# One decoder layer on one core: the last 1,024 rows of the input projection as one stretch, the gated recurrence ahead of the attention, half of the second modulation on VectorE

## Chip, cores and metric

The kernel runs on one core of a Trainium2 chip. The metric is the device time of one execution in microseconds, the median of several runs. All weights are float32 and come from HBM; every weight is used once.

## What is computed

One layer for 256 tokens of width 2048. `c` is one vector; `mod` gives six rows of 2048, each from 2048 x 2048 weights (16 MiB).

```python
mod = silu(c) @ w_ada + b_ada
sh1, sc1, g1, sh2, sc2, g2 = split(mod, 6)
h = rmsnorm(x, norm1_g) * (1 + sc1) + sh1
hq, hf, hi, hg, q_a, kv_a, k_pe = split(h @ w_in)      # 2048 x 4928
o_a = rmsnorm(hgrn2(hq, hf, hi)) * silu(hg)            # gated recurrence, 8 heads
o_b = rmsnorm(attention(q_a, kv_a, k_pe))              # low-rank q and kv up-projections, 8 heads
x = x + g1 * (concat(o_a, o_b) @ w_out)                # 2048 x 2048
h2 = rmsnorm(x, norm2_g) * (1 + sc2) + sh2
x = x + g2 * moe(h2)       # 32 experts, two per token, gate/up/down 2048 x 512
```

## The kernel before

All large weights pass through one ring of SBUF buffers of 2 MiB. A list `items` gives their order; `ring_fill` issues the loads on SP's queue in that order, `ring_get` takes a chunk, `ring_done` gives its buffer back, and the next load is then issued. The ring has four buffers, two more from `close_temps` on and a seventh once the splits' memory is free.

The kinds of items are: `ad1`, the modulation sh1/sc1 for two K tiles a pair of chunks, by TensorE; `adt`, the same for one K tile, by VectorE, in two passes of 128 x 2048 over transposed weights (`adt_chunk`); `ada`, one eighth of one of g1, sh2, sc2, g2 by TensorE (`ada_chunk`, L293), closed by `ada_end`; `wh` and `win`, the input projection for a pair of column blocks; `qup`/`kvup` for half of the attention heads; `wout` for the output projection; then `gu` and `dn` of the experts.

The input projection has ten column blocks in five pairs: (2,3) and (4,5) are the first half of the recurrence's inputs, (6,7) and (8,9) the second, (0,1) those of attention. Its 16 K tiles go in steps: K tiles 0, 1 and 2, 3 (`wh`, all pairs), then 4 to 7, 8 to 11 and 12 to 15 (`win`). `make_h` prepares h for two K tiles as soon as their modulation is known. `dense` does the matmuls: each weight block of 128 x 512 is divided by ScalarE and VectorE into a high and a low part (a split, L417 and L418, four in flight), and six matmuls (twelve at half the width, L425 to L427) use it. After every step the two sums in PSUM are copied or added to `proj` in SBUF (L455, L457).

The order around the change: K tiles 8 to 11 of all pairs, interleaved with `adt`, then for K tiles 12 to 15 the pair (0,1), which starts `mla_pre`, then `qup`/`kvup` 0 (`mla(0)`), (2,3), (4,5), which starts the first recurrence `hgrn(0)`, `mla(1)`, (6,7), (8,9) and `hgrn(1)`. Between them stand the `ada` chunks; `SPREAD` says how many behind each. The output projection takes the attention half of its rows first (`w_out`, half 0), and the recurrence half second. The last three g2 chunks run behind the output projection, while the router is computed; the first experts' chunks stand ahead of them in the ring. The instructions of each engine are ordered by the framework's scheduler from priorities, so that work of later items can stand among that of earlier ones; each engine then works its own line in order.

Of the kernel before, what the change touches and what calls it, by code (L numbers as in the profile page):

```python
# [45 lines left out]
def tile_hybrid_layer(ctx, tc, A, out):  # L46
# [37 lines left out]
    def bc(ap, shape):  # L84
# [20 lines left out]
    ad1 = [("ad1", h, c) for h in range(2) for c in range(2)]  # L105
    adt = [("adt", kt) for kt in range(4, 16)]
    mods = [("ada", b, ch) for b in ("g1", "sh2", "sc2", "g2") for ch in range(8)]
    last = [[("win", 3, (0, 1))], [("qup", 0), ("kvup", 0), ("win", 3, (2, 3))], [("win", 3, (4, 5))],
            [("qup", 1), ("kvup", 1), ("win", 3, (6, 7))], [("win", 3, (8, 9))]]
    last += [[("wout", 0, j)] for j in range(4)]  # L110
    items = ad1[:2]

    def merge(ws, bs):

        done = 0
        for i, w in enumerate(ws):
            items.append(w)
            want = min(len(bs), -(-(i + 1) * len(bs) // len(ws)))
            items.extend(bs[done:want])
            done = want  # L120

    merge([("wh", 0, p) for p in pairs], ad1[2:])
    merge([("wh", 1, p) for p in pairs], adt[:4])
    for q in range(1, 3):
        merge([("win", q, p) for p in pairs], adt[4 * q:4 * q + 4])
    late_mods = iter(mods)
    items = [x for i, it in enumerate(items) for x in [it] + [next(late_mods) for _ in range(EARLY.get(i, 0))]]
    for ws, n in zip(last + [[("wout", 1, j)] for j in range(4)], SPREAD):
        items += ws + [next(late_mods) for _ in range(n)]
    g2 = list(late_mods)  # L130
    experts = [(k, e, q) for e in range(NE) for k, q in (("gu", 0), ("gu", 1), ("gu", 2), ("gu", 3), ("dn", 0), ("dn", 1))]
    items += experts[:HEAD] + g2 + experts[HEAD:]
    index = {it: i for i, it in enumerate(items)}

    def source(it):
# [5 lines left out]
        if k == "wh":  # L141
            if it[2] == (0, 1):
                return A["w_in_1h"][it[1]], 1664
            return A["w_in_h"][it[1], it[2][0] // 2 - 1], 2048
        if k == "ada":
            return A["w_ada"][("g1", "sh2", "sc2", "g2").index(it[1]), it[2]], 4096
        if k == "win":
            if it[2] == (0, 1):
                return A["w_in_1"][it[1] - 1], 3328
            return A["w_in"][it[1] - 1, it[2][0] // 2 - 1], 4096  # L150
# [1056 lines left out]
```

## Time and profile before

| | us |
|---|---|
| median of 3 runs | 1505.96 (1504.96 to 1506.98) |
| the profiled execution | 1505.27 |
| its span | 1503.0 |
| TensorE busy | 1127.9 (75%) |
| VectorE busy | 588.6 (39%) |
| ScalarE busy | 338.4 (23%) |
| DMA, mean | 383 GB/s, 575.61 MB |

The span counts from the first to the last instruction on the core. Shares are means over stages that differ: the dense layers with the modulation fill the first 570 us, the experts the rest. Busy times of matmuls overlap, as they are pipelined: a 512-wide matmul lasts 0.40 us in the records and the next starts 0.23 us after it.

### The profile page before, as it was taken

To read this page: it belongs to the slowest core of one execution; us is meant where nothing else is said; L and a number is where in the kernel's file an instruction comes from. 1 tells how busy PE (TensorE), PEld (TensorE's weight loads), DVE (VectorE), ACT (ScalarE), POOL (GpSimd) and SP (SyncE) were. 2 spreads that over 40 slices of the span, in tenths; PEclk is the share of its full clock that TensorE was granted. 3 is DMA by queue.
4 is the path that set the end of the run, shared out by engine and by line. 5 is a ranking of instruction groups with operands and counts; after the bars stand their busy time and mean duration, and the time that the engine had idled before them with its cause. 6 is when DMAs were issued, how large, how long until landed. Compare 5 with 4: busy or idle time off the path is not lost.

```text
span 1503.0 us, 22846 instructions
## 1 busy us (share of the span) xinstructions
PE 1127.9 (75%) x9893; PEld 687.8 (46%) x9893; DVE 588.6 (39%) x1200; ACT 338.4 (23%) x699; POOL 5.0 (0%) x9
## 2 busy tenths in 40 slices
PE   5989999979999989675666666657657756666556
PEld 2868887737568756333323323323423423332222
DVE  4699998769765552220120121113112112112112
ACT  5634446536435423000100100100100100000000
POOL 0000000000000000000000000000000000000000
PEclk7999999989999999888888888879888889779787
DMA  9788796877979798999999999999999999999995
GB/s 373 263 332 356 298 352 257 315 302 313 369 293 376 293 373 343 430 429 430 430 430 430 430 430 429 429 431 430 430 430 430 430 431 430 430 429 429 431 430 222
DMA packets 44143, 575.61 MB, mean 383 GB/s; under 512 B 4858, under 2 KB 5114, under 8 KB 8712
## 3 DMA queue, kind: packets, MB, share of 16 engines
q1 hardware_dynamic: 42496, 570.56, 91.4%
q10 hardware_dynamic: 1544, 3.56, 0.6%
q8 instruction: 79, 1.29, 0.3%
q14 instruction: 24, 0.20, 0.0%
HBM read 572.00 MB, written 2.11 MB: 382 GB/s over the span
## 4 chain that ended last, share of the span: by engine, by line
DMA 51%; PE 37%; DVE 9%; ACT 1%; issue 1%; SPq 0%; ACTq 0%; DVEq 0%
DMA wch<-in_w_gu_dram 37%; DMA wch<-in_w_down_dram 13%; PE pgu L1040 5%; PE pacc L433 5%; PE pacc L434 5%; PE pacc L432 5%; PE pada L293 3%; PE py L1016 3%; PE pcmb L993 2%; PE pgat L970 2%; DVE wch L271 2%; DVE split L418 2%; DVE proj L457 1%; PE pacc L427 1%; PE pacc L425 1%; PE pacc L426 1%
## 5 line engine op out<-in xcount | busy, mean ns | idle before, releaser
L1040 PE MATMUL pgu<-wch,XT 128*32 128x256 f32 x4096 | 309.7, 455 | 201.0 <-DMA wch<-in_w_gu_dram 201.0
L1040 PEld LDWEIGHTS pgu<-wch,XT 128*32 128x32 f32 x4096 | 139.2, 126 | 361.0 <-DMA wch<-in_w_gu_dram 253.9
L1016 PE MATMUL py<-wch,hT 128*32 128x256 f32 x2048 | 167.9, 485 | 76.8 <-DMA wch<-in_w_down_dram 72.1
L1020 DVE TENSOR_TENSOR Y<-py,gate 32x256 f32<-32x256 f32 x256 | 107.6, 420 | 216.5 <-PE py L1016 213.6
L1005 DVE TENSOR_TENSOR hid<-sgu,pgu 128x128 f32<-128x128 f32 x32 | 9.2, 287 | 462.2 <-ACT sgu L1003 462.2
L418 DVE TENSOR_TENSOR split<-wch,split 128x512 fp32r<-128x512 f32 (+2 forms) x248 | 159.5, 666 | 69.6 <-ACT split L417 69.0
L417 ACT ACTIVATE split<-wch 128x512 fp32r<-128x512 f32 (+2 forms) x248 | 148.0, 614 | 161.2 <-PE pacc L434 98.4
L1016 PEld LDWEIGHTS py<-wch,hT 128*32 128x32 f32 x2048 | 78.9, 133 | 155.0 <-issue 60.8
L1003 ACT ACTIVATE sgu<-pgu 128x128 f32<-128x128 f32 x32 | 8.9, 277 | 602.5 <-PE pgu L1040 602.5
L975 ACT ACTIVATE XT<-pgat,sh,a 128x128 f32<-128x128 f32 x128 | 48.1, 456 | 223.1 <-PE pgat L970 223.0
L433 PE MATMUL pacc<-split,hhi 128*128 128x512 f32 (+1 forms) x192 | 75.5, 393 | 7.0 <-DVE split L418 7.0
L425 PE MATMUL pacc<-hhi,split 128*128 128x256 f32 x256 | 72.4, 286 | 2.8 <-ACT hhi L388 2.2
L426 PE MATMUL pacc<-hlo,split 128*128 128x256 f32 x256 | 72.7, 285 | 1.7 <-DVE hlo L389 1.7
L434 PE MATMUL pacc<-split,hlo 128*128 128x512 f32 (+1 forms) x192 | 73.7, 386 | 0.0
L432 PE MATMUL pacc<-split,hhi 128*128 128x512 f32 (+1 forms) x192 | 72.9, 392 | 0.8 <-DVE proj L457 0.7
L427 PE MATMUL pacc<-hhi,split 128*128 128x256 f32 x256 | 72.2, 285 | 1.1 <-DVE split L418 1.1
L293 PE MATMUL pada<-wch,ca 128*1 128x512 f32 x512 | 68.7, 602 | 3.3 <-DVE pada L288 3.3
L993 PE MATMUL pcmb<-Y,pwt 128*128 128x512 f32 x128 | 59.2, 605 | 15.5 <-DVE Y L1020 15.5
L970 PEld LDWEIGHTS pgat<-ohr,x 128*128 128x128 f32 x512 | 63.4, 205 | 10.7 <-issue 9.8
L970 PE MATMUL pgat<-ohr,x 128*128 128x128 f32 x512 | 66.8, 291 | 0.7 <-DVE sm L937 0.7
L271 DVE SCALAR_TENSOR_TENSOR wch<-wch,gate 128x2048 f32<-128x2048 f32 x24 | 54.8, 2284 | 0.0
L457 DVE TENSOR_TENSOR proj<-proj,pacc 128x512 f32<-128x512 f32 (+1 forms) x80 | 51.2, 662 | 0.8 <-PE pacc L434 0.4
(311 smaller groups left out, 1215.4 us busy)
## 6 DMA issues: line engine op xcount, KB each, us to landing
wch<-in_w_gu_dram SPq DMA_DIRECT2D x128, 2048.0 KB, 31.1
wch<-in_w_down_dram SPq DMA_DIRECT2D x64, 2048.0 KB, 31.5
wch<-in_w_ada_dram SPq DMA_DIRECT2D x36, 2048.0 KB, 10.1
wch<-in_w_ada_t_dram SPq DMA_DIRECT2D x12, 2048.0 KB, 7.9
wch<-in_w_in_dram SPq DMA_DIRECT2D x12, 2048.0 KB, 9.2
wch<-in_w_out_dram SPq DMA_DIRECT2D x8, 2048.0 KB, 9.5
wch<-in_w_in_h_dram SPq DMA_DIRECT2D x8, 1024.0 KB, 8.9
wch<-in_w_in_dram SPq DMA_DIRECT2D x3, 1664.0 KB, 7.0
```

The lines of the kernel that those rows point to most:

```text
L293: PE.matmul(acc[b][32 * j:32 * j + 1, :], ca[:, kt:kt + 1], w[:, o:o + 512], start=kt == 0, stop=kt == 15)
L417: S.activation(s[:, 0, :ncol], w, AF.Copy)
L418: V.tensor_sub(s[:, 1, :ncol], w, s[:, 0, :ncol])
L426: PE.matmul(o, s[:, 0, c], lo, start=False, stop=False, skip_group_check=True)
L432: PE.matmul(o, hi[:, c], s[:, 0, :ncol], start=first, stop=False)
L433: PE.matmul(o, hi[:, c], s[:, 1, :ncol], start=False, stop=False)
L434: PE.matmul(o, lo[:, c], s[:, 0, :ncol], start=False, stop=stop)
L970: PE.matmul(ps[:, 128 * i:128 * i + 128], x2[kt // 4][:, t, 128 * (kt % 4):128 * (kt % 4) + 128], ohr[:, t], start=t == 0, stop=t == 1)
L993: PE.matmul(ps, PWT[G4][:, 128 * t:128 * t + 128], Y4[j // 2][:, 512 * (j % 2):512 * (j % 2) + 512], start=True, stop=True)
L1016: PE.matmul(py[32 * j:32 * j + 32, :256], H["T"][:, 32 * kt:32 * kt + 32], w[:, 1024 * kt + 256 * j:1024 * kt + 256 * j + 256], start=kt = ...
L1020: V.tensor_mul(Y[q][r:r + 32, 256 * j:256 * j + 256], py[32 * j:32 * j + 32, :256], gate[32 * j:32 * j + 32, c:c + 256])
L1040: PE.matmul(gu[32 * j:32 * j + 32, :256], XT[G4][kt // 8][:, kt % 8, 32 * e4:32 * e4 + 32], w[:, 1024 * i + 256 * j:1024 * i + 256 * j + 2 ...
```

## The change

Input projection: only the pairs (2,3) and (4,5) are taken in two halves for K tiles 0 to 3; the other three take the four at once. For K tiles 8 to 15 each pair runs through both steps with its sums left in PSUM: `dense` returns them (`end` is None) and takes them up again, and they are added to `proj` once. So 8 + 20 + 20 sums are added instead of 80.

Order: K tiles 8 to 15 go (2,3), (4,5), `hgrn(0)`, (6,7), (8,9), `hgrn(1)`, (0,1), `mla_pre`, then `mla(0)`, one quarter of the recurrence half of the output projection, `mla(1)`, the rest of that half, and the attention half last.

Modulation: K tiles 14 and 15 of sh1/sc1 move from `adt` to a third pair of `ad1` chunks. The second half of sh2 and sc2 (K tiles 8 to 15) is done on VectorE in eight chunks `at2`, each in eight passes of 128 x 512 at lowered priority; the first halves of sh2 and sc2 together make one row `m2` of eight `ada` chunks. So there are 24 `ada` chunks instead of 32. All stand ahead of the output projection's second half, g2 before g1; none is left for the router's stretch. Besides, the arena has 17 tiles instead of 14, `brows` moves out of it, and a scratch size of the program is set to 1024.

```diff
-RING, NARENA, NTEMP, NSPLIT, RING2 = 4, 14, (8, 6), 4, 2
-SPREAD = (1, 4, 7, 5, 5, 2, 0, 0, 0, 2, 1, 1, 0)
-EARLY = {33: 1}
-HEAD = 2
+RING, NARENA, NTEMP, NSPLIT, RING2 = 4, 17, (8, 6), 4, 2
+SPREAD = (0, 0, 2, 5, 7, 3, 0, 4, 1, 1, 1, 0, 0, 0, 0)
+SPREAD_T = (2, 2, 0, 0, 0, 0, 2, 0, 1, 1, 0, 0, 0, 0, 0)
...
+    items = [ad1(0, 0), ad1(0, 1), ("wh", 0, pairs[0]), ad1(1, 0), ("wh", 0, pairs[1]), ad1(1, 1), adt(4), ("wh", 1, pairs[0]),
+             ("wh", 1, pairs[1]), adt(5)]
+    for k, q, p, a in ((0, 0, 2, 6), (0, 0, 3, 7), (0, 0, 4, 8), (1, 1, 0, 9), (1, 1, 1, 10), (1, 1, 2, 11), (1, 1, 3, 12),
+                       (1, 1, 4, 13)):
+        items += [("win", q, pairs[p]), adt(a)]
+    items += [ad1(2, 0), ad1(2, 1)]
+    steps = [[("win", 2, p), ("win", 3, p)] for p in pairs]
+    steps += [[("qup", 0), ("kvup", 0)], [("wout", 0, 0)], [("qup", 1), ("kvup", 1)]] + [[("wout", 0, j)] for j in range(1, 4)]
+    steps += [[("wout", 1, j)] for j in range(4)]
+    mods = iter([("ada", b, ch) for b in ("m2", "g2", "g1") for ch in range(8)])
+    turned = iter([("at2", kt) for kt in range(8, 16)])
+    for ws, n, m in zip(steps, SPREAD, SPREAD_T):
+        items += ws + [next(turned) for _ in range(m)] + [next(mods) for _ in range(n)]
...
-    items += experts[:HEAD] + g2 + experts[HEAD:]
+    items += experts
...
+    def at2_chunk(i):
+
+        w = ring_get(("at2", i))
+        r = sm(8, "at2")
+        for k in range(8):
+            wk = w[:, 512 * k:512 * k + 512]
+            with tc.high_priority(-60):
+                V.scalar_tensor_tensor(wk, wk, 1.0, gate[:, 512 * (k % 4):512 * (k % 4) + 512], op0=OP.mult, op1=OP.mult,
+                                       accum_out=r[:, k:k + 1])
+        ring_done(("at2", i))
+        t = sm(2, "at2")
+        V.tensor_reduce(t, r.rearrange("p (k i) -> p k i", k=2), AX.X, OP.add)
+        mod_shift(sh2[:, i:i + 1], t[:, 0:1], P_BA + 32 + i, 1)
+        mod_scale(a2[:, i:i + 1], t[:, 1:2], P_BA + 48 + i, P_N2 + i, 1)
...
-    def dense(wt, ncol, kts, lhs, end, turned=False):
+    def dense(wt, ncol, kts, lhs, end, turned=False, ps=None):
-        ps = [pw("pacc") for _ in range(2)]
+        fresh = ps is None
+        if fresh:
+            ps = [pw("pacc") for _ in range(2)]
...
-            first, stop = i == 0, kt == kts[-1]
+            first, stop = fresh and i == 0, kt == kts[-1] and end is not None
...
+        if end is None:
+            return ps
         end(ps)
...
-            dense(wt[:, off:off + len(kts) * ncol], ncol, kts, lhs, end, turned=n in (2, 5, 6, 9))
+            held = dense(wt[:, off:off + len(kts) * ncol], ncol, kts, lhs, None if q == 2 else end, turned=n in (2, 5, 6, 9),
+                         ps=sums.pop(n, None))
+            if q == 2:
+                sums[n] = held
...
-            hi, lo = mixT[2 - 2 * half + kt // 4]
+            hi, lo = mixT[2 * half + kt // 4]
...
-        ("win", 3, (0, 1)): mla_pre,
-        ("win", 3, (4, 5)): lambda: (router_load(), hgrn(0)),
+        ("win", 3, (4, 5)): lambda: hgrn(0),
         ("win", 3, (8, 9)): lambda: hgrn(1),
-        ("ada", "sc2", 7): router_weights,
-        ("wout", 0, 1): close_temps,
+        ("win", 3, (0, 1)): lambda: (router_load(), mla_pre()),
+        ("at2", 15): router_weights,
+        ("wout", 0, 2): close_temps,
...
-    for it in g2:
-        ada_chunk(it[1], it[2])
...
-    nc = bacc.Bacc("TRN2", target_bir_lowering=False, num_devices=1)
+    nc = bacc.Bacc("TRN2", target_bir_lowering=False, num_devices=1, dynamic_dma_scratch_size=1024)
```

## Rows read from the trace of the kernel before

**Rows 1.** The page's slices: the span in 40 slices, busy tenths.

```profile
PE   5989999979999989675666666657657756666556
DVE  4699998769765552220120121113112112112112
PEclk7999999989999999888888888879888889779787
DMA  9788796877979798999999999999999999999995
```

**Rows 2.** Windows: stretch, length; busy us (instructions) by engine; granted clock, DMA share, GB/s.

```profile
31.40:66.30 34.90, 34.84 (x212) 28.40 (x213) 16.48 (x35) 25.29 (x46) 0.00 (x0) 0.92 0.75 277
66.30:167.30 101.00, 90.81 (x536) 77.26 (x535) 97.53 (x161) 43.56 (x76) 0.00 (x0) 0.98 0.87 339
167.30:545.50 378.20, 358.20 (x2179) 260.21 (x2177) 271.54 (x510) 181.82 (x341) 3.81 (x4) 0.98 0.81 319
300.00:320.00 20.00, 12.05 (x81) 4.55 (x83) 16.43 (x28) 6.35 (x10) 0.00 (x0) 0.74 0.82 320
400.00:420.00 20.00, 14.13 (x104) 8.69 (x102) 19.47 (x43) 7.63 (x11) 0.95 (x1) 0.91 0.99 385
545.50:571.40 25.90, 20.42 (x120) 11.72 (x119) 15.23 (x60) 6.70 (x20) 0.00 (x0) 0.80 0.83 334
571.40:1484.00 912.60, 597.91 (x6745) 301.61 (x6748) 163.15 (x371) 65.69 (x190) 0.00 (x0) 0.84 1.00 426
```

**Rows 3.** The page's costliest groups: two of VectorE; busy us, mean ns, idle before.

```profile
L271 DVE SCALAR_TENSOR_TENSOR wch<-wch,gate 128x2048 f32<-128x2048 f32 x24 | 54.8, 2284 | 0.0
L457 DVE TENSOR_TENSOR proj<-proj,pacc 128x512 f32<-128x512 f32 (+1 forms) x80 | 51.2, 662 | 0.8 <-PE pacc L434 0.4
```

**Rows 4.** Line 330, a pass of 512 with accumulator: duration ns min/median/max, starts.

```profile
L330 DVE SCALAR_TENSOR_TENSOR junk<-x x4: 684/692/694, 12.9 to 16.8; 128x512 f32<-128x512 f32 x4
L330 DVE DVE_READ_ACCUMULATOR junk<-x x4: 82/82/84, 13.5 to 17.4; 128x1 f32 x4
```

**Rows 5.** TensorE's timeline: start, us, line, count, [idle before, releaser].

```profile
31.46 0.80 PE L425 MATMUL pacc<-hhi,split 128*128 128x256 f32 x2 [2.25 <-ACT hhi L388]
...
308.96 1.97 PE L824 MATMUL pmt<-cst,o 128*128 128x128 f32 x8 [4.63 <-DVE o L818]
314.25 4.04 PE L293 MATMUL pada<-wch,ca 128*1 128x512 f32 x18 [3.32 <-DVE pada L288]
...
415.67 1.75 PE L520 MATMUL ptr<-cst,d 128*128 128x128 f32 x8 [5.15 <-DVE d L513]
...
512.25 1.90 PE L293 MATMUL pada<-wch,ca 128*1 128x512 f32 x16
...
535.03 0.40 PE L433 MATMUL pacc<-split,mhi 128*128 128x512 f32 x1
535.26 0.40 PE L434 MATMUL pacc<-split,mlo 128*128 128x512 f32 x1
```

**Rows 6.** Waits of SP's queue over the span: us in total, times, longest.

```profile
SPq L172 <- PE pada L293: 173.4, 32, 19.5
...
SPq L172 <- DVE wch L271: 45.3, 12, 11.3
```

**Rows 7.** Timeline of the router's stretch, VectorE and the first expert matmuls.

```profile
554.97 0.68 DVE L302 TENSOR_TENSOR brows<-brows,pada 1x512 f32<-1x512 f32 x1 [0.56 <-PE pada L293]
555.57 0.14 DVE L884 TENSOR_REDUCE mx<-lg 128x2 f32<-128x8 f32 x1
...
558.49 0.17 DVE L890 TENSOR_TENSOR eq<-cst,ft 128x8 f32<-128x8 f32 x1
...
559.16 0.22 DVE L884 TENSOR_REDUCE mx<-el 128x2 f32<-128x64 f32 x1
...
560.18 0.22 DVE L890 TENSOR_TENSOR eq<-cst,ft 128x64 f32<-128x64 f32 x1
...
571.41 1.93 PE L1040 MATMUL pgu<-wch,XT 128*32 128x256 f32 x32
```

**Rows 8.** A window of 3 us ahead of the first expert, columns as in rows 2.

```profile
569.00:572.00 3.00, 3.00 (x32) 2.71 (x35) 0.00 (x0) 1.98 (x6) 0.00 (x0) 0.92 0.05 22
```

More of the change, by code (lines that the diff above doesn't have):

```diff
@@ L104, in tile_hybrid_layer @@
     pairs = [(2, 3), (4, 5), (6, 7), (8, 9), (0, 1)]
[L105 to L127, printed above, removed]
@@ L128, in tile_hybrid_layer @@
-    for ws, n in zip(last + [[("wout", 1, j)] for j in range(4)], SPREAD):
-        items += ws + [next(late_mods) for _ in range(n)]
-    g2 = list(late_mods)
+    ad1 = lambda h, c: ("ad1", h, c)
+    adt = lambda kt: ("adt", kt)
+    items = [ad1(0, 0), ad1(0, 1), ("wh", 0, pairs[0]), ad1(1, 0), ("wh", 0, pairs[1]), ad1(1, 1), adt(4), ("wh", 1, pairs[0]),
[3 more added lines that the diff above has]
+        items += [("win", q, pairs[p]), adt(a)]
@@ L131, in tile_hybrid_layer @@
+    assert not list(mods) and not list(turned)
     experts = [(k, e, q) for e in range(NE) for k, q in (("gu", 0), ("gu", 1), ("gu", 2), ("gu", 3), ("dn", 0), ("dn", 1))]
-    items += experts[:HEAD] + g2 + experts[HEAD:]
+    items += experts
     index = {it: i for i, it in enumerate(items)}
@@ L260, in ad1_chunk @@
             PE.matmul(ps[:, n:n + 1], rows[:, 128 * n:128 * n + 128], ones[:, 0:1], start=True, stop=True)
-        mod_shift(sh1[:, 2 * h:2 * h + 2], ps[:, 0:2], P_BA + 2 * h, 2)
-        mod_scale(a1[:, 2 * h:2 * h + 2], ps[:, 2:4], P_BA + 16 + 2 * h, P_N1 + 2 * h, 2)
+        k = (0, 2, 14)[h]
+        mod_shift(sh1[:, k:k + 2], ps[:, 0:2], P_BA + k, 2)
+        mod_scale(a1[:, k:k + 2], ps[:, 2:4], P_BA + 16 + k, P_N1 + k, 2)
     def adt_chunk(i):
@@ L405, in forget_bound @@
         V.tensor_scalar(lbc[:, 8:16], lbc[:, 0:8], -1.0, 1.0, op0=OP.mult, op1=OP.add)
-    proj = {}
-    def dense(wt, ncol, kts, lhs, end, turned=False):
-        ps = [pw("pacc") for _ in range(2)]
+    proj, sums = {}, {}
+    def dense(wt, ncol, kts, lhs, end, turned=False, ps=None):
+        fresh = ps is None
+        if fresh:
+            ps = [pw("pacc") for _ in range(2)]
         for i, kt in enumerate(kts):
@@ L851, in tile_hybrid_layer @@
             adt_chunk(it[1])
+        elif it[0] == "at2":
+            at2_chunk(it[1])
         elif it[0] == "ada":
@@ L1169, in _layout @@
                 t[q, p, :, k] = w[:, 4 * q:4 * q + 4, cols[2 + 2 * p + k]]
-    L["w_in"] = t.reshape(4, 4, P, 4096)[1:]
-    L["w_in_h"] = ac(t[0].reshape(4, P, 2, 2, 2, 512).transpose(3, 0, 1, 2, 4, 5)).reshape(2, 4, P, 2048)
-    L["w_in_1h"] = np.stack([np.concatenate(
-        [w[:, 2 * h:2 * h + 2, cols[k]].reshape(P, -1) for k in range(2)], axis=1) for h in range(2)])
+    L["w_in"] = t.reshape(4, 4, P, 4096)
+    L["w_in_h"] = ac(t[0, :2].reshape(2, P, 2, 2, 2, 512).transpose(3, 0, 1, 2, 4, 5)).reshape(2, 2, P, 2048)
     L["w_in_1"] = np.stack([np.concatenate(
-        [w[:, 4 * q:4 * q + 4, cols[k]].reshape(P, -1) for k in range(2)], axis=1) for q in range(1, 4)])
+        [w[:, 4 * q:4 * q + 4, cols[k]].reshape(P, -1) for k in range(2)], axis=1) for q in range(4)])
     w = np.asarray(i["w_q_up"])[0].reshape(4, P, 2, 4, 192)
```

38 lines of the change are left out of this document (19 added, 19 removed).

## The prediction

> **What bounds the kernel now.** I read the slices of the span first, then cut the span into stages. The slices [rows 1] show two halves. From slice 17 on the DMA row stands at 9 and TensorE at about 6. Before that TensorE stands at 9 almost everywhere and the DMA row swings between 6 and 9. The stage table [rows 2] puts numbers on it: from 571.4 to 1484 us, the experts, the DMA share is 1.00 at 426 GB/s. The weights of the 32 experts do not change, so that stage and its tail cost the same once the first expert's matmuls can start with the ring full. What the change can move is the time of that start, 571.4 us [rows 7].
>
> Up to there it is TensorE's stage. From 31.4 us, when the first projection matmul starts, to 545.5 us, when the last output-projection matmul ends, TensorE is busy 34.84 + 90.81 + 358.20 = 483.9 of 514.1 us; 30.2 us are idle [rows 2]. The idle time has three homes: 10.2 us between 66.3 and 167.3, where VectorE is busy 97.53 of 101 us; 8.0 us in 300 to 320 and 5.9 us in 400 to 420; and 6.2 us scattered. The two holes are single waits of 4.63, 3.32 and 5.15 us for VectorE steps of attention and recurrence [rows 5], at places where runs of seven or five modulation chunks stand in TensorE's line and no projection work. In these holes the DMA share is 0.82 and 0.99: no weights could come faster. Elsewhere the DMA idles because the ring's four buffers are held: the queue waited 173.4 us in 32 waits for TensorE to get to modulation chunks [rows 6].
>
> So the account of the profiled execution is 31.4 + 483.9 + 30.2 + 25.9 (router) + 931.6 (experts and end) = 1503.0 us of span, and 2.3 us around it give its 1505.27, which is 0.7 below the median of the runs. I leave 31.4, 931.6 and 2.3 as they are.
>
> **TensorE's work.** A modulation chunk costs 16 matmul records in 1.90 us [rows 5]. Before, 29 of the 32 lie ahead of 545.5 us and three in the router stretch. After, 24 are left, all ahead: 5 x 1.90 = 9.5 us less. The third pair of ad1 chunks (K tiles 14 and 15) adds two of the same shape, at full clock 2 x 1.9 = 3.8 us. Held sums change no matmul. Net **-5.7 us** of busy time. The low clock in the two holes (0.74 and 0.91 [rows 2]) goes with them if they go: at most 0.26 x 20 + 0.09 x 20 = 7 us could come from that, but only what ran slowly is regained; I take **-2**, between 0 and -4.
>
> **VectorE's work.** Removed: the sums onto proj fall from 80 to 48 (8 for the two halved pairs, 20 for K tiles 4 to 7, 20 for the held stretch), 32 x 0.66 = 21 us [rows 3]. Two adt chunks go, 4 x (2.28 + 0.08) plus small steps, 10 us [rows 3, 4]. Added: 64 short passes. The trace has no in-place pass of 512 over a weight chunk; the nearest row is the same operation at 128x512 with an accumulator, 0.69 us and 0.08 for the accumulator read [rows 4]; the other end is a quarter of the 2048 pass, 0.57. I take the former: 64 x 0.77 = 49 us (lower end 37), plus 5 us of reductions and small adds. Net +23 us. Where it falls matters more. From 167.3 on VectorE was busy 271.5 of 378.2 us [rows 2]; there the change takes away 21 (the last four adt chunks) and 13 (20 of 40 sums) and adds 54: 292 us, in some 365: 80%. Ahead of 167.3 us it was nearly full; 8 us of sums go, two more adt chunks are now due there (+10). So the first part stays VectorE's: no gain in its 10.2 us, and two ad1 chunks and two more preparations of h (about 6 us of TensorE work) move into it from later.
>
> **Waits that the order adds or removes.** (1) Start: only two of the five pairs are halved now. In the old order the pairs after (4,5) covered ad1's way through ScalarE, TensorE, VectorE and ScalarE before the second half can start; I price that by the same way to the first matmul at 31.46 us, whose last wait alone is 2.25 us [rows 5]; the whole way is some 4 us. Bounds 0 and 5; taken +3. (2) Behind the first recurrence now stand the pairs (6,7) and (8,9), 32 splits of six matmuls 0.23 us apart [rows 5], 45 us of TensorE work, and behind the second the pair (0,1), 19 us, where the old line had modulation chunks alone. The 13.9 us of holes should go. (3) In their place stands a run of seven modulation chunks between (0,1) and the query projection, with five more shortly before. From there to the second projection's end the ring must bring 5 + 7 chunks of 2 MiB, 3.25 MiB of (0,1) and 2.5 MiB: 31.2 MB, 73 us at the experts' 426 GB/s. TensorE has in the same stretch 12 x 1.9 = 23 us of modulation, 19 us for (0,1) and the second recurrence with the preparation of attention, which I put at 15: 57 us. Four buffers ahead are worth 8.4 MB, 20 us. So 53 against 57: covered with nothing to spare. Bounds 0 and 13 us idle; I take 5. (4) The g1 rows now end just ahead of the second half of the output projection. The two DMAs that spread them over the partitions are issued by ScalarE and wait for VectorE's four adds, for the last short pass (which reads the old gate) and for each other; ScalarE's splits queue behind them, and TensorE behind those. Up to four finished splits lie ahead, 4 x 6 matmuls, 5.6 us of cover. Cost 0 while the last at2 chunk is done by then; otherwise what it is late. (5) The scattered 6.2 us: with VectorE at 80% instead of 72% I take 7. (6) The router loads, now behind the second recurrence, and x2's loads on SP's queue keep their cover: 0.
>
> Idle after: 13 + 5 + 7 = 25 us, **-5** against 30.2; from 10 (all cover holds) to 52.
>
> **Router.** The three g2 chunks leave it. VectorE's first maximum ran from 555.57 to 558.49 us because four g2 adds of 0.69 us stood between its steps; the same steps run from 559.16 to 560.18 later [rows 7]: 1.9 us. The first add itself stands 0.6 us ahead, and TensorE's transposes waited up to 0.9 us behind g2 chunks. Taken **-3**, between 0 and -4. The ring's seven buffers are full in either case before the first expert starts: the DMA share is down to 0.05 in 569 to 572 us [rows 8], and without the g2 chunks it fills sooner.
>
> **Sum:** -5.7 - 2 - 5 - 3 = -15.7 us: 1505.3 - 15.7 = **1490 us**. Best ends together -34 (1471); worst: -5.7 + 22 = +16 (1521).
>
> **One rule weighed.** In 300 to 320 us TensorE was busy 12.05 us at a granted 0.74, a mix of the levels 1.2 and 2.4 GHz, behind waits of 3 to 5 us [rows 2, 5]. The Trainium skill (TensorE: Matmul & The Clock Gate, "HAM oscillation") says that short groups of matmuls with waits for weights between them start cold each time. That speaks against the seven chunks in a row; the rows agree with it at the old place.
>
> **Rivals.**
> First, the stage stays as full as it is (the forecast's work less, no idle won, the clock as before): -5.7 - 3 + up to 9 of new VectorE waits, 1497 to 1506. For it: VectorE is full ahead of 167 us and gets more in all. Against: its share after that is only 80%. Chance 0.18, time 1501.
> Second, **slower**: at2 chunks hold the ring. A chunk that VectorE takes in eight low-priority passes keeps one of four buffers until the last. For the longer passes the queue waited 45.3 us in 12 waits, the longest 11.3 us [rows 6]. Three times two at2 chunks stand together; the two free buffers then hold two chunks of eight splits, 2 x 8 x 6 x 0.233 = 22.4 us of TensorE work. It decides where each is held for more than 11 us past its turn: if the eight are 5 us later than that, TensorE loses 8 x 5 = 40 us, less the 15.7: +24, 1530; at 3 us, +8, 1514. Against: VectorE has the room on the mean. Chance 0.15, time 1514.
> Third, the run of seven is paced by the DMA after all and the clock drops in it: 13 us idle instead of 5, and the 5 us that a granted 0.74 cost in 20 us: +13, 1503. Chance 0.07.
> Fourth, held sums need all four matmul buffers of a pair at once, so the change does not give one stretch without stops: if each of the five pairs waits for two sums of 0.69 us, +7, 1497. Against: the first column's buffers are free 5.6 us before. Chance 0.04.
>
> **How the numbers follow.** Forecast 1490, chance 0.56. The range 1471 to 1514 leaves about 0.1 on each side: below only if every cover holds, above if at2 chunks block badly. This kernel's runs agree so that about 0.2% (3 us) can be told from no change. Faster: the forecast 0.56, of the first rival 0.10, of the third 0.04, the fourth 0.04: 0.74. Same: 0.07 of the first and 0.03 of the third, 0.10. Slower: the second 0.15 and 0.01 of the first, 0.16.
>
> **What would show it.** Right: first expert matmul (line of pgu) at about 556 us instead of 571; modulation matmuls before it 384 records instead of 464; the holes ended by VectorE steps of attention or recurrence gone; VectorE busier by 20 us or so; the expert stage 912 to 915 us at DMA share 1.00. Wrong: SP's queue waiting long for the short passes, ScalarE's splits idle behind DMAs of weights, or a granted clock well below 0.9 ahead of the query projection. If the experts' stage changed its length, the account itself would be wrong.

## The result, and the profile after

The changed kernel takes **1552.01 us** (median of 4, 1551.63 to 1553.82) against 1505.51 for the kernel before in the same comparison: a ratio of **1.031, 95% interval 1.0292 to 1.0328**. The forecast was 1490 and faster; the change costs 46.5 us.

The page's slices of the kernel after, to be read against [rows 1]: busy tenths of 40 slices.

```profile
PE   6898997987878987866656666667566666667555
DVE  4679797744786755212112112112112112112112
PEclk7999999999889998989888889888988889887878
DMA  9887974779647974999999999999999999999995
```

A slice is 38.8 us. TensorE's row of nines has 6, 7 and 8 in it now, and the DMA row falls to 4 in slices 7, 12 and 16. TensorE and the transfers both got emptier: neither took the other's place as the bound. The DMA row stands at 9 for good from slice 17 on, as before, but that is 620 us now and was 601.

Windows of the kernel after, columns as in [rows 2]: the stage up to the last output projection matmul, the router, the experts, then parts of the first.

```profile
31.65:596.65 565.00, 492.33 (x2880) 374.60 (x2880) 404.06 (x822) 244.73 (x457) 3.81 (x4) 0.94 0.77 302
596.65:619.29 22.64, 14.29 (x71) 11.98 (x71) 12.42 (x56) 6.62 (x20) 0.00 (x0) 0.70 0.25 93
619.30:1531.00 911.70, 593.52 (x6745) 301.37 (x6748) 163.23 (x371) 65.76 (x189) 0.00 (x0) 0.85 1.00 426
...
31.65:175.50 143.85, 128.47 (x752) 108.20 (x756) 116.14 (x194) 67.86 (x118) 0.00 (x0) 0.94 0.82 319
345.00:420.00 75.00, 60.61 (x355) 35.92 (x354) 44.29 (x111) 26.76 (x68) 0.95 (x1) 0.89 0.89 362
...
240.00:260.00 20.00, 15.12 (x106) 11.86 (x104) 15.52 (x46) 7.30 (x13) 0.00 (x0) 0.99 0.15 45
...
440.00:460.00 20.00, 10.71 (x51) 8.69 (x52) 18.70 (x60) 9.05 (x20) 0.00 (x0) 0.74 0.53 190
...
248.60:262.50 13.90, 6.53 (x45) 5.40 (x43) 13.90 (x44) 3.80 (x6) 0.00 (x0) 0.89 0.40 141
439.00:453.00 14.00, 5.35 (x33) 3.84 (x31) 13.72 (x45) 6.26 (x13) 0.00 (x0) 0.79 0.27 85
...
192.00:213.00 21.00, 18.20 (x96) 15.19 (x95) 19.95 (x53) 11.37 (x17) 0.00 (x0) 0.92 0.79 319
500.00:521.00 21.00, 19.00 (x101) 12.22 (x99) 20.27 (x62) 8.83 (x18) 0.00 (x0) 1.00 0.84 322
```

The first expert matmul starts at 619.29 us (571.41 before, [rows 7]). The account used in the prediction closes on it: start 31.65 for 31.46; TensorE busy 492.3 for 483.9 (**+8.4**); idle 565.0 - 492.3 = 72.7 for 30.2 (**+42.5**); router 22.6 for 25.9 (**-3.3**); experts and end 1550.2 - 619.3 = 930.9 for 931.6. Together +47 us of span. So the loss is idle time of TensorE ahead of the output projection's end, and 8 us more of busy time at a lower granted clock (0.94 over the stage).

The 64 passes stand in four groups of 16, and the last four windows are at these groups. 248.60 to 262.50 and 439.00 to 453.00 show the idle time at its worst: in 27.9 us VectorE is busy 27.6 us, TensorE 11.9 us, so 16.0 us are idle in these two places alone. In the two other groups, the last two windows, splits stand among the passes, and TensorE is busy 18.2 and 19.0 of 21 us. VectorE's timeline of the kernel after, through the group at 248.60:

```profile
247.96 0.69 DVE L423 TENSOR_TENSOR split<-wch,split 128x512 fp32r<-128x512 f32 x1
248.56 0.16 DVE L188 TENSOR_TENSOR sm<-sm 128x8 f32<-128x8 f32 x1
248.64 0.69 DVE L273 SCALAR_TENSOR_TENSOR wch<-wch,gate 128x512 f32<-128x512 f32 x1
...
254.20 0.69 DVE L273 SCALAR_TENSOR_TENSOR wch<-wch,gate 128x512 f32<-128x512 f32 x1
254.81 0.09 DVE L273 DVE_READ_ACCUMULATOR wch<-wch,gate 128x1 f32 x1
254.81 0.69 DVE L273 SCALAR_TENSOR_TENSOR wch<-wch,gate 128x512 f32<-128x512 f32 x1
...
261.92 0.69 DVE L273 SCALAR_TENSOR_TENSOR wch<-wch,gate 128x512 f32<-128x512 f32 x1
...
262.53 0.69 DVE L423 TENSOR_TENSOR split<-wch,split 128x512 fp32r<-128x512 f32 x1
```

Between the split at 247.96 and the next at 262.53 stand all 16 passes of two at2 chunks, mixed with steps of the recurrence's end. Where two follow each other they start 0.61 us apart. TensorE's timeline of the kernel after has the other end, and with it the three longest waits behind 175.5 us (start, us, line; idle before and releaser):

```profile
263.27 0.80 PE L438 MATMUL pacc<-split,hhi 128*128 128x512 f32 x1 [7.77 <-DVE split L423]
...
368.43 3.43 PE L298 MATMUL pada<-wch,ca 128*1 128x512 f32 x16 [3.58 <-DMA wch<-in_w_ada_dram]
...
454.00 0.58 PE L438 MATMUL pacc<-split,qahi 128*128 128x256 f32 x1 [7.01 <-DVE split L423]
...
556.43 0.79 PE L438 MATMUL pacc<-split,mhi 128*128 128x512 f32 x1 [6.46 <-DVE split L423]
```

The wait of 6.46 us has another cause than the passes, as VectorE's line just ahead of it shows:

```profile
554.48 1.29 DVE L593 TENSOR_TENSOR mix<-mix,gate 128x512 f32<-128x512 f32 x2 [6.69 <-DMA gate<-grow]
```

The first product with the new gate (g1) waits there 6.69 us for the DMA that spreads the row over the partitions, and the next splits stand behind it in VectorE's line.

And SP's queue: its timeline first, then its waits over the span (us in total, times, longest).

```profile
203.29 9.11 SPq L161 DMA_DIRECT2D wch<-in_w_ada_t_dram  x2
217.04 13.41 SPq L161 DMA_DIRECT2D wch<-in_w_in_dram  x2
256.15 6.82 SPq L161 DMA_DIRECT2D wch<-in_w_ada_dram  x2
```

```profile
SPq L161 <- PE pada L298: 101.1, 22, 17.5
SPq L161 <- DVE wch L273: 71.9, 6, 25.6
```

The two at2 chunks were asked for at 203.29 and 212.07 us, and VectorE began the first at 248.64. Nothing was issued from 230.45 until the first was given back at 256.15. That is the 0.15 of DMA share in 240 to 260 above. With a median of 9.5 us from issue to landing for these two loads, each of the two buffers stood full and unused for some 36 us. At 368.43, in the run of seven modulation chunks, TensorE waits for a load.

### The profile page after: what moved, and what is told of

Same layout as the page of the kernel before. It is cut to its first block, busy times and chain, and to the rows that moved or that the text cites. A ratio compares the mean times of both kernels' runs of the same rounds, so it can differ in the third digit from the quotient of the medians.

```text
span 1550.2 us, 22732 instructions
## 1 busy us (share of the span) xinstructions
PE 1127.9 (73%) x9801; PEld 697.8 (45%) x9801; DVE 604.5 (39%) x1316; ACT 332.6 (21%) x695; POOL 5.0 (0%) x9
## 5 line engine op out<-in xcount | busy, mean ns | idle before, releaser
L1050 PE MATMUL pgu<-wch,XT 128*32 128x256 f32 x4096 | 303.8, 448 | 197.1 <-DMA wch<-in_w_gu_dram 192.7
L430 PE MATMUL pacc<-hhi,split 128*128 128x256 f32 x256 | 74.8, 294 | 6.4 <-ACT split L422 4.6
L432 PE MATMUL pacc<-hhi,split 128*128 128x256 f32 x256 | 73.8, 293 | 6.6 <-DVE split L423 6.6
L1005 PE MATMUL pcmb<-Y,pwt 128*128 128x512 f32 x128 | 63.1, 638 | 15.5 <-DVE Y L1032 15.5
L438 PE MATMUL pacc<-split,mhi 128*128 128x512 f32 x128 | 52.8, 412 | 8.5 <-DVE split L423 8.5
L298 PE MATMUL pada<-wch,ca 128*1 128x512 f32 x384 | 52.5, 613 | 8.2 <-DMA wch<-in_w_ada_dram 6.6
L430 PEld LDWEIGHTS pacc<-hhi,split 128*128 128x128 f32 x256 | 51.2, 201 | 8.6 <-ACT split L422 5.7
## 6 DMA issues: line engine op xcount, KB each, us to landing
wch<-in_w_out_dram SPq DMA_DIRECT2D x8, 2048.0 KB, 15.6
x<-in_x_dram SPq DMA_DIRECT2D x8, 512.0 KB, 11.2
```

The source lines that it names most:

```text
L430: PE.matmul(o, s[:, 0, c], hi, start=first and h % 2 == 0, stop=False, skip_group_check=True)
L432: PE.matmul(o, s[:, 1, c], hi, start=False, stop=stop, skip_group_check=True)
L438: PE.matmul(o, hi[:, c], s[:, 1, :ncol], start=False, stop=False)
L1050: PE.matmul(gu[32 * j:32 * j + 32, :256], XT[G4][kt // 8][:, kt % 8, 32 * e4:32 * e4 + 32], w[:, 1024 * i + 256 * j:1024 * i + 256 * j + 2 ...
```

## Experiments

The theory: the 64 passes on VectorE cost the time, by standing late (a held buffer) and in blocks (splits and steps of the branches behind them). The rivals: the order bunches the modulation chunks, so that the transfers come unevenly; the recurrence first is the worse order; the new start or the held sums cost something. Medians and ratios are to the kernel before, run beside each.

**1. No at2: the fourth row on TensorE.** at2 becomes a row `m3` of eight `ada` chunks in the same places of the list.

```diff
-    mods = iter([("ada", b, ch) for b in ("m2", "g2", "g1") for ch in range(8)])
-    turned = iter([("at2", kt) for kt in range(8, 16)])
+    mods = iter([("ada", b, ch) for b in ("m3", "m2", "g2", "g1") for ch in range(8)])
+    turned = iter([])
-        items += ws + [next(turned) for _ in range(m)] + [next(mods) for _ in range(n)]
+        items += ws + [next(mods) for _ in range(n + m)]
```

> The changed kernel with the second half of sh2 and sc2 back on TensorE: a fourth row of eight ada chunks; the number of modulation chunks behind each item is the same, and so are the bytes; all else stays. VectorE loses 49 us of passes, TensorE gains 8 x 1.9 = 15 us. Theory A: 1500 to 1518 us, at least 34 us gained. Theory B: 1540 to 1560 us, as the bytes come in the same bunches.

1534.98 us, 1.0199 (1.0182 to 1.0216): 17 us come back although TensorE does 8 x 1.9 = 15 us more. Its window of the same place:

```profile
240.00:260.00 20.00, 20.00 (x144) 15.55 (x145) 11.34 (x19) 9.50 (x17) 1.92 (x2) 1.00 0.74 286
```

TensorE is full and the DMA share is 0.74 instead of 0.15. The time lies between the two ranges. So at2 is a cause, and not the only one: 29 us are left.

**2. The passes at another priority.** If low priority makes them late, a higher one moves them.

```diff
-            with tc.high_priority(-60):
+            with tc.high_priority(0):
```

> The changed kernel with one edit: the short passes of at2 lose their lowered priority and stand in VectorE's line where the order of the items puts them. Theory A (late passes hold ring buffers, up to 25.6 us in one wait of SP's queue, and stand in blocks ahead of splits): the waits of SP's queue for the passes fall from 72 us to under 30 us, TensorE's two waits of 7 to 8 us behind blocks of passes go, and the time falls from 1552 to 1515 to 1530 us. Theory B (the order bunches bytes: pairs of projection chunks with nothing between them, then runs of five to seven modulation chunks, so that the DMA first idles and then paces TensorE): it stays at 1543 us or more, with the DMA share at 0.3 or below around 300 to 320 us as in the changed kernel.

1557.54 us, 1.0343 (1.0326 to 1.0360). With 600 instead of 0:

> The changed kernel with the short passes raised far ahead in priority, so that in VectorE's line they stand in front of the recurrence's and attention's steps, where lowering or leaving their priority put them behind (that moved nothing: 1552 and 1558 us). Theory A1 (what costs is that the passes stand behind the branch's steps and hold ring buffers till then): SP's queue waits under 30 us for them instead of 72, and the time is 1520 to 1535 us. Theory A2 (what costs is VectorE's 49 us themselves, wherever they stand): SP's waits fall, and the time stays 1545 us or more.

1558.06 us, 1.0338 (1.0321 to 1.0355). The first pass of the same block, first with 0, then with 600:

```profile
249.97 0.68 DVE L273 SCALAR_TENSOR_TENSOR wch<-wch,gate 128x512 f32<-128x512 f32 x1
```

```profile
252.09 0.68 DVE L273 SCALAR_TENSOR_TENSOR wch<-wch,gate 128x512 f32<-128x512 f32 x1
...
261.27 0.68 DVE L273 SCALAR_TENSOR_TENSOR wch<-wch,gate 128x512 f32<-128x512 f32 x1
```

Against 248.64: with three priorities the group starts at nearly the same time. The number does act inside the group: with 600 the 16 passes from 252.09 to 261.27 stand in one row with nothing between them, and with -60 and 0 steps of the recurrence stand among them. The waits of SP's queue for the passes stay at 71.6 and 58.0 us, so neither run tests what a pass that stands early would cost. What they show is that the lowered priority isn't the cause. That the scheduler places a group by when it reckons the load to be there is an inference.

**3. The other way round: at2 alone in the kernel before.** Eight at2 chunks take the place of the first modulation row; the rest of the kernel before stays.

```diff
-    mods = [("ada", b, ch) for b in ("g1", "sh2", "sc2", "g2") for ch in range(8)]
+    mods = [("at2", kt) for kt in range(8, 16)] + [("ada", b, ch) for b in ("m2", "g1", "g2") for ch in range(8)]
```

> The kernel before with one part of the change alone: second half of sh2 and sc2 on VectorE in the same short passes at the same lowered priority. As the passes read the old gate, the eight at2 chunks take the places of the first modulation row, then come m2, g1 and g2. Theory A: SP's queue waits 30 us or more for the passes and the kernel is 15 to 35 us slower than before, 1520 to 1540. Theory B: 1495 to 1510 us, since the order of bytes is that of before.

1556.01 us, 1.0332 (1.0314 to 1.0349): at2 alone costs as much as the whole change, more than the range of Theory A. Its queue of SP, and its window at the hole of [rows 2]:

```profile
SPq L174 <- DVE wch L285: 75.8, 7, 36.4
```

```profile
300.00:320.00 20.00, 4.92 (x20) 3.75 (x20) 16.51 (x49) 8.60 (x14) 0.00 (x0) 0.56 0.21 75
```

In this list four at2 chunks stand in a row behind (2,3) and the chunks of the first attention half, which makes it a hard case for them; the size isn't to be carried over.

**4. Held sums undone.** Every step adds its sums to `proj` again.

```diff
-            held = dense(wt[:, off:off + len(kts) * ncol], ncol, kts, lhs, None if q == 2 else end, turned=n in (2, 5, 6, 9),
-                         ps=sums.pop(n, None))
-            if q == 2:
-                sums[n] = held
+            held = dense(wt[:, off:off + len(kts) * ncol], ncol, kts, lhs, end, turned=n in (2, 5, 6, 9))
```

> The changed kernel with one part undone: the sums of the last 1,024 rows are added to proj after each of the two steps again (20 more sums of 0.66 us on VectorE, 13 us). If held sums cost anything (four matmul buffers taken by one pair): 1535 to 1546 us. If they are a plain relief of VectorE, which is what I take from the changed kernel, where no wait of TensorE ends on a sum into proj for more than 1 us: 1553 to 1566 us.

1560.53 us, 1.0368 (1.0349 to 1.0387): 8.5 us slower, VectorE busy 414.87 us in the stage for 404.06. The held sums are a gain of their own.

**5. The start of the kernel before** (all five pairs halved, third ad1 pair kept).

```diff
-    items = [ad1(0, 0), ad1(0, 1), ("wh", 0, pairs[0]), ad1(1, 0), ("wh", 0, pairs[1]), ad1(1, 1), adt(4), ("wh", 1, pairs[0]),
...
+    for i, p in enumerate(pairs):
+        items += [("wh", 1, p), adt(4 + i)]
+    for i, p in enumerate(pairs):
+        items += [("win", 1, p), adt(9 + i)]
```

> The changed kernel with the old start: all five pairs take K tiles 0 to 3 in two halves again, so that the way of ad1's second pair is covered by three more halves; 12 more sums on VectorE (8 us). TensorE's idle time up to 170 us is 15.4 us in the changed kernel against about 10 before. If the start loses those: 1540 to 1547 us. If VectorE is the bound there and the 12 sums weigh as much: 1550 to 1560 us.

1554.89 us, 1.0317 (1.0296 to 1.0339): no difference that can be told. The start isn't the cause.

**6. Order and evenness.** Three choices are crossed: recurrence or attention first, modulation chunks bunched as in the change or one to three behind every chunk of the projection, at2 or the fourth row on TensorE. The core of the edits (attention first, then even):

```diff
-    steps = [[("win", 2, p), ("win", 3, p)] for p in pairs]
+    two = lambda p: [("win", 2, pairs[p]), ("win", 3, pairs[p])]
+    steps = [two(4), [("qup", 0), ("kvup", 0)] + two(0), two(1), [("qup", 1), ("kvup", 1)] + two(2), two(3)]
...
-SPREAD = (0, 3, 7, 5, 5, 1, 1, 1, 1, 0, 0, 0, 0)
+SPREAD = (1, 3, 2, 1, 2, 2, 3, 2, 2, 2, 2, 2, 2, 2, 2, 2, 0, 0, 0, 0)
```

> The changed kernel with the old order of the branches: (0,1) and attention first, the recurrences after (4,5) and (8,9), the attention half of the output projection first; held sums and at2 stay, modulation chunks stand behind the items about as in the kernel before, at2 in pairs behind the first two and then one behind each quarter of the output projection. If the order of the branches is what costs (the attention's waits now fall where TensorE has little else): 1520 to 1540 us. If it is the passes: 1545 to 1570 us.

> The changed kernel with the ada chunks spread out: one or two behind each projection chunk of the last 1,024 rows, between the two steps of a pair too, instead of none behind the first two pairs and runs of five and seven later; at2 chunks and their lowered priority stay, two behind the same pairs. Theory A: the passes still hold buffers, 1535 us or more, and SP's queue still waits 60 us or more for them. Theory B: 1500 to 1525 us, and no stretch of 20 us with a DMA share under 0.4 between 200 and 460 us.

> The kernel with at2 back on TensorE (1535 us), with all 32 ada chunks spread out, one or two behind each projection chunk, between the two steps of a pair too. With the passes gone the bunching of bytes can show: it has the DMA share at 0.46 to 0.48 in two stretches of 20 us and at 1.00 in three. Theory B (bunched bytes are the rest of the loss): 1505 to 1522 us. If the rest lies in the waits of the branches: 1528 to 1545 us.

> Two parts undone together: second half of sh2 and sc2 on TensorE (alone 17 us better) and attention ahead of the recurrence (alone 9 us better), held sums and the new start stay. If the two losses are separate: 1552 - 17 - 9, 1520 to 1531 us. If both undo the same loss (at2 chunks behind the first recurrence): 1533 to 1545 us. If the rest of the way to 1505 lies in their combination: under 1515 us.

> As the kernel with both parts undone, with the 32 modulation chunks spread out, one to three behind each projection chunk, none behind the last four quarters of the output projection. If bunching still costs once the passes are gone (3 us with the recurrence first): 3 to 12 us under the run with both undone. It is also the candidate to beat the kernel before, as it keeps the held sums, which are worth 8 us: under 1505 us if nothing else of the change costs.

> The changed kernel with attention first and its modulation chunks spread out as in the run at 1512 us, but with at2 on VectorE: the same number of chunks behind each item, eight of them at2 (five behind the first four steps, two and one behind the third and fourth quarter of the output projection). If the passes cost only where bytes are bunched: 1512 to 1520 us. If VectorE's passes cost by themselves: 1526 to 1545 us.

| order, modulation chunks | with at2 | fourth row on TensorE | cost of at2 |
|---|---|---|---|
| recurrence first, bunched | 1552.0 (the change) | 1535.0 | 17 |
| recurrence first, even | 1563.4, 1.0375 (1.0358 to 1.0393) | 1531.6, 1.0168 (1.0151 to 1.0185) | 32 |
| attention first, bunched | 1543.4, 1.0263 (1.0238 to 1.0288) | 1536.9, 1.0206 (1.0189 to 1.0223) | 6 |
| attention first, even | 1541.1, 1.0226 (1.0209 to 1.0243) | **1512.4**, 1.0042 (1.0028 to 1.0056) | 29 |

Two of the six missed their ranges: attention first alone (1543.4) fell between its two, and evenness without at2 and with the attention first gained 25 us where 3 to 12 were expected.

The three don't add up. Evenness is worth 25 us, but only with the attention first and without at2; with at2 and the recurrence first it costs 11. The recurrence first costs 9 to 22 us but for one pair, the bunched rows without at2, which agree within 2. at2 costs something in all four, and most where the chunks are spread evenly. So the share of each part depends on the order in which they are put in. From the best cell to the change one way gives at2 29, bunching 2, recurrence first 9; another gives recurrence first 19, bunching 3, at2 17.

The last line of the table holds the cleanest pair: modulation chunks at the same places, with and without the passes (only the router's weights are prepared behind another chunk). Windows of the kernel with at2 (attention first, even):

```profile
201.00:218.00 17.00, 8.15 (x47) 5.01 (x45) 17.00 (x64) 6.36 (x20) 0.00 (x0) 0.80 0.62 198
275.70:288.00 12.30, 6.53 (x36) 3.11 (x34) 12.30 (x42) 3.50 (x4) 0.00 (x0) 0.88 0.40 141
498.10:522.00 23.90, 17.46 (x69) 13.49 (x68) 21.34 (x67) 6.55 (x11) 0.00 (x0) 0.86 1.01 429
```

The same windows of the kernel without:

```profile
201.00:218.00 17.00, 14.92 (x93) 7.69 (x92) 12.17 (x37) 8.94 (x26) 0.00 (x0) 1.00 0.96 390
275.70:288.00 12.30, 12.30 (x92) 9.19 (x88) 10.40 (x19) 6.12 (x9) 0.00 (x0) 1.00 0.96 378
498.10:522.00 23.90, 22.84 (x92) 18.00 (x91) 13.24 (x21) 10.05 (x17) 0.00 (x0) 0.93 1.01 431
```

In the first two windows VectorE is full and TensorE about half idle; in the third VectorE is busy 21.3 of 23.9 us. In these 53.2 us TensorE is idle 21.1 us with at2 and 3.1 without. SP's waits for at2 chunks in the kernel with at2 (two lines, as some are put down to the small step behind the passes):

```profile
SPq L161 <- DVE at L277: 17.7, 5, 5.4
...
SPq L161 <- DVE wch L273: 5.4, 1, 5.4
```

Those are 23 us in six waits, none above 5.4, for 72 us and 25.6 in the changed kernel. A third line, of the additions (`a`, L285), has 15.6 us here and 6.2 in the kernel without, so it may hide 9 more, in one wait. at2 costs more here although the queue waits much less for it. That speaks for the blocks on VectorE's line as the larger price and the held ring as the smaller. It compares two orders, and no run here takes the one away and leaves the other.

**7. One pass behind each split.** The order of the last cell, each pass written by hand behind one split. The edit also moves three of the eight at2 chunks: they stand behind (4,5) and the second half of the attention heads, eight or nine places ahead of where the last cell has them (behind the third and fourth quarter of the output projection).

```diff
+    def one_pass():
+        if passes and next(passes[0]) == "done":
+            passes.pop(0)
+            one_pass()
...
-            with tc.high_priority(-60):
...
+            if k < 7:
+                yield
```

> The order of at2_attention_even (1541.1 us; the same order with the fourth ada row instead of at2, tensor_attention_even, 1512.4), with the same eight at2 chunks and 64 passes of 0.69 + 0.08 us, but each pass is written by hand behind one split of the projection steps that follow, at ordinary priority, one pass a split, and the at2 chunks stand one step earlier. All of the layer is computed. Theory A, the passes cost because VectorE's line takes 8 to 16 of them in a block of 5 to 13 us ahead of splits and branch steps: with a pass at a time most of the 29 us come back, 1512 to 1522, and the windows in which TensorE was busy about 10 of 20 us (200 to 220 and 280 to 300) stand above 16. Rival, VectorE's 49 us of work cost the same wherever they stand, or each buffer is held longer for being taken in 64 short steps: 1530 or more, with TensorE's waits for splits and SP's waits for wch spread instead of bunched.

1556.33 us, 1.0336 (1.0318 to 1.0353). By the number the rival holds, but the edit didn't give what it was to test. VectorE's timeline:

```profile
202.10 0.69 DVE L274 SCALAR_TENSOR_TENSOR wch<-wch,gate 128x512 f32<-128x512 f32 x1
...
206.64 0.69 DVE L274 SCALAR_TENSOR_TENSOR wch<-wch,gate 128x512 f32<-128x512 f32 x1
...
207.25 0.17 DVE L674 TENSOR_SCALAR sm<-sm 128x2 f32<-128x2 f32 x1
...
207.39 0.69 DVE L274 SCALAR_TENSOR_TENSOR wch<-wch,gate 128x512 f32<-128x512 f32 x1
...
209.72 0.69 DVE L274 SCALAR_TENSOR_TENSOR wch<-wch,gate 128x512 f32<-128x512 f32 x1
...
210.33 0.49 DVE L682 TENSOR_SCALAR proj<-proj,sm 128x512 f32<-128x512 f32 x1
```

The written order was not kept. Eleven passes still stand between 202.10 and 210.41, one between almost every two small steps of the query's norm, a chain of steps of 0.16 us each of which waits for the one before. TensorE waits for its end just as in the kernel of the last cell (6.41 us there, at 209.81):

```profile
210.87 1.11 PE L686 MATMUL pqa<-cst,proj 128*128 128x128 f32 x4 [6.40 <-DVE proj L682]
```

SP's waits for at2 chunks are nearly all in one line:

```profile
SPq L161 <- DVE at L280: 14.9, 3, 8.6
```

TensorE is busy 10.4 of 20 us from 200 to 220 and 9.9 from 280 to 300, where the theory wanted 16. The queue waits no longer for at2 chunks than in the last cell, and the kernel is 15 us slower. As three chunks stand elsewhere, these 15 us can't be put down to the passes' new form. Whether 64 passes that really stand one by one among splits would be cheap stays open; no run here got them there.

**8. A fifth buffer of the ring.** 14 arena tiles leave the memory for it.

```diff
-RING, NARENA, NTEMP, NSPLIT, RING2 = 4, 17, (8, 6), 4, 2
+RING, NARENA, NTEMP, NSPLIT, RING2 = 5, 14, (8, 6), 4, 2
```

> The changed kernel with five ring buffers instead of four and 14 arena tiles instead of 17, nothing else. If held buffers starve the DMA (A1): a fifth gives two runs of at2 and pairs room, 1515 to 1535 us, with the DMA share in 240 to 265 us above 0.5 (0.31 in the changed kernel). If VectorE's load is the cost (A2): 1545 us or more. The smaller arena can cost by itself, so a slower time would not tell.

1542.79 us, 1.0245 (1.0228 to 1.0262): 9 us of the 46, between the two ranges. The sign that was to show the relief is missing: from 240 to 265 us the DMA share is 0.27 (0.31 in the changed kernel). TensorE is still idle 62 us in the stage. In the profiled executions the first expert starts 5.8 us earlier (613.5 for 619.3), and from there to the end it takes 924.5 us for 930.9. So about half of what the fifth buffer brings lies in the experts, where no at2 chunk is left (experiment 9).

**9. Can the rest of the change gain?** Without at2, attention first, even, with the held sums and the third ad1 pair: first all pairs halved, then five buffers, then both; and the kernel before with nothing but five buffers (and the scratch size of the change).

> The run at 1512 us (passes on TensorE, attention first, chunks spread out) with all five pairs in halves for K tiles 0 to 3 again. If the start holds the rest of the loss: 1503 to 1508 us. In the changed kernel this edit made 3 us more; if the start is neutral: 1511 to 1517 us.

> The run at 1512 us with five ring buffers instead of four and 14 arena tiles instead of 17. If four buffers are what makes TensorE and DMA wait for each other: 1490 to 1505 us, faster than the kernel before. If the order is even enough for four: 1509 to 1520 us.

> The kernel before with five ring buffers instead of four, in the memory that the small scratch size frees; all else as before. If held buffers matter in its order too: 1485 to 1500 us, and it is the fastest of all. If its interleaved order makes do with four: 1502 to 1509 us.

> No at2 (four ada rows on TensorE), the attention first, the ada chunks spread evenly, the held sums and the third ad1 pair kept (tensor_attention_even 1512.4); with the start of the kernel before, all five pairs halved (alone: 1510.6), and with five ring buffers for four (alone: 1502.0). All of the layer is computed. If the two gains have different places, they add: 1512.4 - 1.8 - 10.4 = 1500. If the fifth buffer already covers what the halved pairs cover at the start: 1502. Beside it the kernel before with five buffers took 1501.65, so a time of 1502 says that the third ad1 pair, the held sums and the order together are worth nothing once the ring is as long; 1497 or less says that they are worth 5 us.

| | us | ratio (95%) |
|---|---|---|
| all pairs halved | 1510.60 | 1.0026 (1.0015 to 1.0036) |
| five buffers | 1502.00 | 0.9968 (0.9955 to 0.9980) |
| both | 1501.89 | 0.9976 (0.9967 to 0.9986) |
| the kernel before, five buffers | **1501.65** | 0.9961 (0.9947 to 0.9975) |

All three with five buffers are 0.2 to 0.4% faster than the kernel before, and can't be told from each other: on top of the longer ring nothing that is left of the change is worth anything that shows. The kernel before with five buffers fell between its two ranges, and the halved pairs alone 0.4 us below the second of theirs. Window of the experts in the kernel before with five buffers:

```profile
575.74:1482.00 906.26, 593.00 (x6749) 300.14 (x6752) 163.23 (x371) 65.76 (x189) 0.00 (x0) 0.85 1.00 426
```

The first expert starts at 575.74 us, 4.3 later than before, and yet the profiled span is 1.9 us shorter (the medians are 4.9 apart): from there to its end it takes 1501.1 - 575.7 = 925.4 us for 931.6. With another ring the experts' 931.6 us are no constant, as I had them. In the four kernels with five buffers this part takes 924.5 to 926.9 us, in the other sixteen 929.2 to 932.7. The bytes that the DMA moves in it say why; the kernel before first, then the same with five buffers:

```profile
DMA packets 27793, 391.07 MB, mean 420 GB/s; under 512 B 3024, under 2 KB 3024, under 8 KB 4048
DMA packets 27649, 388.97 MB, mean 420 GB/s; under 512 B 3008, under 2 KB 3008, under 8 KB 4032
```

One buffer of 2 MiB, 2.1 MB, less is left to move when the first expert starts, as the longer ring holds one more chunk by then. At 420 GB/s that is an estimated 5 us of a part that the transfers pace. So most of the fifth buffer's gain in the kernel before, and about half of it in the changed one, is a shorter way through the experts and no sign of a ring that is held less in the stage ahead.

## Why the prediction was wrong, point by point

- **The account held.** Start, router and experts came out at +0.2, -3.3 and -0.7 for 0, -3 and 0. The router's term was right: without the g2 chunks it takes 22.6 us. That the experts are a constant holds only while the ring stays as long as it is (experiment 9).
- **TensorE's work held, its clock did not.** The modulation matmuls ahead of the router are 384 records, as forecast, and the stage has 2880 records for 212 + 536 + 2179 = 2927 [rows 2]. Yet busy time rose by 8.4 us where -7.7 was summed. The granted clock over the stage is 0.94, for 0.92 to 0.98 in the three stretches of [rows 2], and 0.74 in 440 to 460, a mix of 1.2 and 2.4 GHz. The holes moved and grew, and the clock fell where they are: the rule weighed was right on the mechanism. The Trainium skill (TensorE: Matmul & The Clock Gate, "HAM oscillation") ties cold starts to matmul groups with waits between; the windows 248.6 to 262.5 and 439 to 453 agree, at 0.89 and 0.79.
- **VectorE's work held.** Busy 404.06 us in the stage for 16.48 + 97.53 + 271.54 = 385.55 [rows 2], +18.5 for "+23"; behind 175.5 us it did 287.9 us where 292 were reckoned, a share of 68% of a stage that had grown. A pass takes 0.69 us with 0.08 for the accumulator, as the nearest row said [rows 4]; as passes in a row overlap, the 64 keep the engine busy 41.9 us and not 49, so that the sum came out near is in part luck.
- **The step that failed** is "VectorE has the room on the mean". From "292 us, in some 365: 80%" I concluded that 64 passes of low priority would fill gaps. In two of their four groups they did, among splits. In the two others the 16 passes and the last steps of a branch fill 14 us of VectorE's line without a split of the next chunk. The cover that I had worked out myself, four splits or 5.6 us, is shorter than such a block. The idle term was 25 us and is 72.7; with the passes off VectorE 17 us of the time come back in this order (experiment 1).
- **A second step that failed** is (4), the g1 rows, a term at 0 "while the last at2 chunk is done by then". The last pass ended at 519.6 us, and the first of the two DMAs was issued at 537.92. Yet TensorE waited 6.46 us. The path was another: ScalarE's wait of 3.3 us for the first DMA cost TensorE nothing that shows, but the second landed 11.2 us after its issue (4.8 in the kernel before), in a window with a DMA share of 1.02 (540 to 560 us), and VectorE's product with the new gate stood ahead of the splits. With at2 on TensorE the wait at this place is still 4.07 us.
- **Its parts.** Ahead of 175.5 us 15.4 us are idle, for 13: right. From 345 to 420, around the run of seven, 14.4 us for 5: the size of the third rival's 13, with the DMA share at 1.01 from 360 to 380; but only 5.0 us of it are waits for loads, and 3.9 are a wait for a step of the attention. All else, for which 7 us were taken, is 72.7 - 15.4 - 14.4 = **42.9 us**: 14.8 in the two waits behind passes, 6.5 in the one for the new gate, the rest in waits of under 3 us.
- **The second rival** (at2 chunks hold the ring) had the right sign and a right link: the queue waited up to 25.6 us, past the 11 from which it was to decide. But it had 0.15 and 1514, and the splits that stand behind a block of passes, 7.77 and 7.01 us of TensorE's idle time, were not in it.
- **The order of the stages** was priced as a gain: "the 13.9 us of holes should go". The old waits for `o`, `pada` and `d` [rows 5], 5.4, 3.3 and 5.1 us in the stage before, fell to 1.9, 0 and 1.4; others came. The recurrence first is 9 to 22 us slower in three of four pairs. Of the 19 us between the two even kernels without at2, idle time has 13 (40.6 for 27.8) and busy time 12 (503.4 for 491.4, clock 0.96 for 0.98), and the router's stretch is 4 us shorter; why this order leaves more gaps isn't settled. So of the 46.5 us 17 come back with at2 alone undone and another 23 when order and evenness are undone too; 6 stay. Why those 23 are lost stays open beyond the waits named here. The third ad1 pair and the smaller parts of the change (arena, `brows`) were not tried by themselves.
- **Held sums** need no four buffers at once at a price: undone, the kernel is 8.5 us slower. The fourth rival falls.

## What to carry to other kernels

A mean share of 80% says how much work fits on an engine, not where it will stand. Before work is given to an engine that feeds another, reckon the longest block that it can form in that engine's line against the cover of the engine behind it (here 10 us of passes against 5.6 us of finished splits), and check in the trace where priority or the written order puts it. Test a many-part change part by part: here the held sums gained 8 us in the changed kernel and at2 lost 6 to 32, depending on the order around it, and one more buffer in the kernel before did as well as the best mix of the parts. And cut the time of a run by stages before naming what gained: the fifth buffer was tried for one stage, and a great part of its gain came in another.

## What the runs showed of the hardware

- Passes in a row start 0.61 us apart, though each lasts 0.69 and has an accumulator read of 0.08 behind it: the ends overlap, so 64 in a row would take an estimated 39 us of the line, not the 49 of the sum; as they stand in the kernel after, they take 41.9.
- A hole in TensorE's line costs more than itself. Behind the wait of 7.77 us at 263.27 six matmuls of 512 start 0.43 us apart, where 0.23 is usual. In all eleven kernels with at2 the clock granted over the stage is 0.92 to 0.94, in the nine without it, the kernel before among them, 0.96 to 0.98. In the cleanest pair TensorE is busy 493.1 us with at2 and 491.4 without, although 8 x 1.9 = 15 us of work were taken from it.
- The same small DMA takes longer to land where the transfers are full. The one that spreads g1 over the partitions landed 4.8 us after its issue at 316.5 us in the kernel before, with a DMA share of 0.94 behind it, and 10.3 to 11.9 us after in the nine kernels that take the recurrence first, with 0.98 to 1.01. Which part of the difference the load makes was not tested by itself.
